# Longer VectorE operations in the state-space sections, and a step between small ScalarE products and the matmuls that read them

## The chip, the cores and the metric

One core of a Trainium2 chip runs the whole kernel, from inputs in HBM to the output in HBM. The metric is the device time of one execution in microseconds, the median of three runs. An execution of which a profile was taken gives the trace.

## What is computed

Two transformer blocks with batch 1, 256 tokens, width 2048, all in float32. The change touches the first block:

```python
mod = cond @ w_ada[i] + b_ada[i]
shift1, scale1, gate1, shift2, scale2, gate2 = jnp.split(mod, N_MOD, axis=-1)
h = _modulate(_rms(x, norm1_w[i]), shift1, scale1)
u, q, k, v = jnp.split(h @ w_in[i], splits, axis=-1)
y_ssm = _s5_mixer(u, ...)              # 64 groups of 64 complex states, a scan over 256 tokens
y_att = _dilated_attention(q, k, v, ...)
x = x + gate1 * (jnp.concatenate([y_ssm, y_att], axis=-1) @ w_out[i])
h2 = _modulate(_rms(x, norm2_w[i]), shift2, scale2)
x = x + gate2 * ((silu(h2 @ w_ffn_gate[i]) * (h2 @ w_ffn_up[i])) @ w_ffn_down[i])
```

The mixer's recurrence is h[t] = abar h[t-1] + bu[t] with complex abar for each state. y_ssm is then y * sigmoid(y @ w_glu). The second block (two attentions, a memory attention and an FFN) is not touched.

## The kernel before

**Weight tiles.** Every weight matrix comes as tiles of 128 x 4 x 512 floats (1 MB) over SP's queue (L199). Float32 products are made of three reduced ones: split_half takes a half tile apart into h (ScalarE, L207) and the residual l (VectorE, L208), and mm3 multiplies (L221, L222, then L226 with l): 24 matmuls of 512 columns a tile. The rows of w_ada come as tiles too; each is reduced with cond by one long VectorE operation (L948).

**The order.** The program order is written out by hand, and every engine works its instructions off in that order. Flow.run goes through the list of tiles. It splits tile n+1, gives tile n to main(), which makes its matmuls, and then calls step() once. step() advances every side task to its next yield (a task with rate 3: three yields). So one step is one weight tile, and what a task issues in a step stands on its engines behind the matmuls of tile n. Where main() needs something that no task has made yet, until() makes steps without tiles.

**The side tasks of the first block.** s_prep makes the tables of the state-space sections. params() computes powers of abar (E8, eight powers for all 32 pairs of groups, by three doublings in double()). Then prep(s) for each of eight sections of four pairs: the products X (L627, L635) and C, their transposes xt, the 64 powers E of the section (a copy of E8's part, L676, and three doublings, L609 to L612), the diagonal dI (L682); a section waits until section s-2 has been run. finish() multiplies out T and makes the section ready. s_run runs up to two ready sections at a time, in steps: input matmuls S and a product with E (L721 to L727), eight scans of 64 elements, one for each part and pair (L732), a product with E (L734 to L737), the output matmuls and gelu (L741 to L747), transposes (L750). When all sections are through, s_run makes glu_acts, which the w_glu tiles read. s_heads1 runs the eight attention heads; the w_out tiles read these, w_out's part 2 heads 0 to 3 before the four w_glu tiles, part 3 heads 4 to 7 behind them.

s_norm1 scales x by its rms (scaled(), L978) and in the same step transposes and modulates it: modulate() calls chunks() with ab, where ScalarE writes h (L262) and f (L263) for each chunk of 128 and VectorE the residual (L264). norm2 uses the same path with another transpose (L240). ada_end makes the gates: four ScalarE products of the identity build a diagonal (L960), a matmul with ones spreads it over the rows (L962), ScalarE copies the row (L964), and then the same again for the second diagonal of the call. There are four such calls, two for gate 2 and two for gate 5.

Of the kernel before, what the change touches and what calls it, by code (L numbers as in the profile page):

```python
# [10 lines left out]
F32 = mybir.dt.float32  # L11
F32R = mybir.dt.float32r
AF = mybir.ActivationFunctionType
OP = mybir.AluOpType
# [9 lines left out]
SP = 4  # L24
# [126 lines left out]
class Core:  # L151
# [94 lines left out]
    def chunks(self, src, n=4, w=None, ab=None, dg=None):  # L246


        nc = self.nc
        out = []  # L250
        for k in range(0, n, 2):
            ps = self.tr4(src, k, dg)
            h, l = self.acts2()
            if w is None and ab is None:
                self.split(ps, h, l)
            for j in range(2):
                if w is not None:
                    self.split(ps[:, j], h[:, j], l[:, j], w(k + j))
                elif ab is not None:
                    a, b = ab(k + j)  # L260
                    f = self.up.tile([128, 256], F32, name=self.nm("f"), tag="f", bufs=3)
                    nc.scalar.activation(h[:, j], ps[:, j], AF.Identity, scale=a, bias=b)  # L262
                    nc.scalar.activation(f, ps[:, j], AF.Identity, scale=a, bias=b)  # L263
                    nc.vector.tensor_tensor(l[:, j], f, h[:, j].bitcast(F32), op=OP.subtract)  # L264
                out.append((h[:, j], l[:, j]))
        return out

# [171 lines left out]
class Ssm:  # L439
    def __init__(self, k, a, pool):  # L440
        self.k, self.a, self.pool = k, a, pool
        nc = k.nc
        self.p = pool.tile([128, 4, 32], F32, name="ssm_p")
        nc.sync.dma_start(self.p, a["ssm_p"])
        self.i32 = pool.tile([128, 32], F32, name="i32")
        nc.gpsimd.tensor_copy(self.i32, k.ident[:, 0:32])
        for q in range(1, 4):
            nc.gpsimd.tensor_tensor(self.i32, self.i32, k.ident[:, 32 * q:32 * q + 32], op=OP.add)
        self.X = pool.tile([128, 2, SP, 4, 32], F32, name="X")
        self.C = [pool.tile([128, 2, SP, 5, 32], F32, name=f"C{i}") for i in range(3)]  # L450
        for t in [self.X] + self.C:
            nc.gpsimd.memset(t, 0.0)
        self.sec = {}
        self.done = self.complete = -1
        self.late = None

    def params(self):

        k, nc = self.k, self.k.nc
        V = nc.vector  # L460
# [133 lines left out]
        yield  # L594
        G = nc.gpsimd
        self.E8 = self.pool.tile([128, 2, 32, 8], F32, name="E8")
        G.memset(self.E8[:, 0, :, 0:1], 1.0)
        G.memset(self.E8[:, 1, :, 0:1], 0.0)
        self.double(self.E8, slice(0, 32), (0, 1, 2))
        yield  # L600

    def double(self, E, pr, steps):

        G, m = self.k.nc.vector, E.shape[2]
        for i in steps:
            n = 1 << i
            u, v = [self.small(2 * m * n).rearrange("p (i a b) -> p i a b", i=2, a=m) for _ in range(2)]
            b = [x[:, pr].unsqueeze(1).unsqueeze(3).to_broadcast([128, 2, m, n]) for x in self.ph[i]]
            G.tensor_tensor(u, E[:, :, :, 0:n], b[0], op=OP.mult)  # L609
            G.tensor_tensor(v, E[:, :, :, 0:n], b[1], op=OP.mult)  # L610
            G.tensor_tensor(E[:, 0, :, n:2 * n], u[:, 0], v[:, 1], op=OP.subtract)
            G.tensor_tensor(E[:, 1, :, n:2 * n], u[:, 1], v[:, 0], op=OP.add)  # L612

    def small(self, n=256):
        return self.pool.tile([128, 256], F32, name=self.k.nm("v"), tag="v32", bufs=4)[:, :n]

    def prep(self, s):
# [55 lines left out]
            A.activation(xt[i], ps, AF.Copy)  # L673
        yield
        E = k.unit((128, 2, SP, 64))
        A.activation(E[:, :, :, 0:8], self.E8[:, :, pr], AF.Copy)  # L676
        self.double(E, pr, (3, 4))
        yield
        self.double(E, pr, (5,))
        yield  # L680
        dI = self.small(SP * 32).rearrange("p (a b) -> p a b", a=SP)
        G.tensor_tensor(dI, self.i32.unsqueeze(1).to_broadcast([128, SP, 32]),  # L682
# [29 lines left out]
    def run(self, s, u4, ytok):  # L712
# [13 lines left out]
        V.tensor_tensor(a[:, 0], a[:, 0], b[:, 1], op=OP.add)  # L726
        V.tensor_tensor(a[:, 1], a[:, 1], b[:, 0], op=OP.subtract)  # L727
        yield
        for i in range(2):
            for q in range(SP):  # L730
                m = self.m4[:, s * SP + q:s * SP + q + 1].to_broadcast([128, 64])
                V.tensor_tensor_scan(b[:, i, q], m, a[:, i, q], initial=0.0, op0=OP.mult, op1=OP.add)  # L732
        yield
        V.tensor_tensor(a, b, eb[0], op=OP.mult)  # L734
        V.tensor_tensor(c, b, eb[1], op=OP.mult)
# [20 lines left out]
def build(ctx, tc, A, out):  # L756
    nc = tc.nc
# [195 lines left out]
    def ada_end(i, half):  # L953
        if i in gate:
            yield
            for j in range(2):
                d = (unit if i == 2 else unit2)((128, 4, 128))
                for c in R4:
                    n = 8 * half + 4 * j + c
                    S.activation(d[:, c], k.ident, AF.Copy, scale=md[i][:, n:n + 1])  # L960
                ps = k.pm()
                PE.matmul(ps, k.ones, d.rearrange("p a b -> p (a b)"), start=True, stop=True)  # L962
                row = (unit if i == 2 else unit2)()
                S.activation(row, ps, AF.Copy)  # L964
                gate[i].append(row)
            return
        yield
        if i in (1, 4):
# [19 lines left out]
    def s_norm1():  # L988
# [13 lines left out]
        for g in R4:  # L1002
            xs = scaled(g, r1)
            x[g] = [None, None]
            while (0, g // 2) not in got or (1, g // 2) not in got:
                yield
            acts1[g] = modulate(xs, g, 0)
            yield
# [626 lines left out]
```

## Time and profile before

| | |
|---|---|
| runs | 2713.55, 2709.04, 2713.08 us, median 2713.08 |
| profiled execution | 2711.92 us, span 2710.1 us |
| TensorE busy | 2616.3 us, 97% |
| VectorE busy | 1670.5 us, 62%, 2124 instructions |
| ScalarE busy | 1269.8 us, 47%, 1818 instructions |
| GpSimd busy | 98.6 us, 4% |
| HBM | 213 GB/s over the span |

Busy time is the union of an engine's instructions. Instructions of one engine overlap in the trace: the next one starts before the last one has ended, so that the distance between two starts is shorter than a duration. An idle time is put down to the instruction whose end released the waiting one. Shares over the whole span mix stages that differ, so the rows below are given by stage.

### The profile page before, as it was taken

To read this page: it belongs to the slowest core of one execution; us is meant where nothing else is said; L and a number is where in the kernel's file an instruction comes from. 1 tells how busy PE (TensorE), PEld (TensorE's weight loads), DVE (VectorE), ACT (ScalarE), POOL (GpSimd) and SP (SyncE) were. 2 spreads that over 40 slices of the span, in tenths; PEclk is the share of its full clock that TensorE was granted. 3 is DMA by queue.
4 is the path that set the end of the run, shared out by engine and by line. 5 is a ranking of instruction groups with operands and counts; after the bars stand their busy time and mean duration, and the time that the engine had idled before them with its cause. 6 is when DMAs were issued, how large, how long until landed. Compare 5 with 4: busy or idle time off the path is not lost.

```text
span 2710.1 us, 31194 instructions
## 1 busy us (share of the span) xinstructions
PE 2616.3 (97%) x12144; PEld 2171.3 (80%) x12144; DVE 1670.5 (62%) x2124; ACT 1269.8 (47%) x1818; POOL 98.6 (4%) x103
## 2 busy tenths in 40 slices
PE   8889989888999999999999999999999999999998
PEld 6778777776877888888888878888888888888887
DVE  7987999878766554554465454655554544455445
ACT  5465446553644344433445554555544433443434
POOL 2000000100000000000000021100000000000001
PEclk9999999999999999999999999999999999999999
DMA  8988765667676555555545434454455555555552
GB/s 348 362 289 328 307 244 215 253 225 297 256 277 232 200 196 190 186 194 195 186 168 192 171 130 162 166 200 171 178 215 197 186 189 196 191 186 186 187 198 96
DMA packets 90147, 578.98 MB, mean 214 GB/s; under 512 B 10000, under 2 KB 12432, under 8 KB 22672
## 3 DMA queue, kind: packets, MB, share of 16 engines
q1 hardware_dynamic: 80928, 561.61, 55.8%
q10 hardware_dynamic: 9072, 15.38, 1.7%
q8 instruction: 95, 1.56, 0.2%
q14 instruction: 52, 0.43, 0.0%
HBM read 570.67 MB, written 6.29 MB: 213 GB/s over the span
## 4 chain that ended last, share of the span: by engine, by line
PE 79%; DVE 15%; ACT 2%; issue 2%; DMA 1%; POOL 0%; ACTq 0%; DVEq 0%; POOLq 0%
PE g L226 24%; PE g L221 24%; PE g L222 24%; DVE l L208 4%; DVE r L948 4%; PE m L238 2%; DVE v L627 1%; ACT h L207 1%; DVE C L635 0%; PE m L342 0%; PE m L1484 0%; PE m L1471 0%; DVE u L732 0%; PE m L240 0%; PE m L226 0%
## 5 line engine op out<-in xcount | busy, mean ns | idle before, releaser
L208 DVE TENSOR_TENSOR l<-r,h 128x1024 fp32r<-128x1024 f32 x866 | 1028.5, 1223 | 573.6 <-ACT h L207 568.0
L221 PE MATMUL g<-h,u 128*128 128x512 f32 x3424 | 1352.6, 395 | 8.8 <-ACT h L207 6.5
L222 PE MATMUL g<-h,u 128*128 128x512 f32 x3424 | 1338.2, 391 | 0.0
L207 ACT ACTIVATE h<-r 128x1024 fp32r<-128x1024 f32 x866 | 884.1, 1056 | 625.1 <-PE g L222 593.0
L226 PE MATMUL g<-l,u 128*128 128x512 f32 x3424 | 922.2, 391 | 33.0 <-DVE l L208 33.0
L226 PEld LDWEIGHTS g<-l,u 128*128 128x128 f32 x3424 | 643.2, 189 | 178.3 <-DVE l L208 45.6
L221 PEld LDWEIGHTS g<-h,u 128*128 128x128 f32 x3424 | 647.9, 189 | 144.8 <-ACT h L207 10.2
L222 PEld LDWEIGHTS g<-h,u 128*128 128x128 f32 x3424 | 648.0, 189 | 132.4 <-issue 1.0
L948 DVE CUSTOM_DVE_ANT_0 r<-r,cond,vec 128x2048 f32<-128x2048 f32 x96 | 224.5, 2343 | 0.2
L271 ACT ACTIVATE u<-m 128x512 fp32r<-128x512 f32 (+1 forms) x80 | 42.7, 574 | 164.1 <-PE m L238 128.3
L272 DVE TENSOR_TENSOR u<-m,u 128x512 fp32r<-128x512 f32 (+1 forms) x80 | 50.0, 658 | 86.6 <-ACT u L271 86.5
L291 ACT ACTIVATE j<-u 128x512 bf16<-128x512 f32 (+2 forms) x92 | 47.3, 514 | 118.2 <-DVE u L1204 31.2
L238 PE MATMUL m<-ident,u 128*128 128x128 f32 x372 | 53.4, 287 | 19.8 <-POOL base_e L488 7.1
L274 ACT ACTIVATE u<-m,vec 128x256 fp32r<-128x256 f32 x86 | 38.9, 472 | 69.8 <-PE m L342 30.8
L275 DVE SCALAR_TENSOR_TENSOR u<-m,vec,u 128x256 fp32r<-128x256 f32 x86 | 40.0, 481 | 48.2 <-ACT u L274 48.1
L238 PEld LDWEIGHTS m<-ident,u 128*128 128x128 f32 x372 | 45.9, 148 | 27.5 <-ACT u L978 8.7
L299 POOL TENSOR_TENSOR r<-s,mhalf 128x2 f32<-128x2 f32 x5 | 5.5, 1102 | 1098.7 <-DVE s L298 1098.7
L1251 DVE TENSOR_TENSOR w<-g,w 128x512 f32<-128x512 f32 x24 | 16.5, 687 | 43.1 <-PE g L226 43.1
L1235 DVE SCALAR_TENSOR_TENSOR w<-g,r,w 128x512 f32<-128x512 f32 x22 | 15.5, 747 | 44.4 <-PE g L226 44.4
L1233 DVE TENSOR_TENSOR w<-g,w 128x512 f32<-128x512 f32 x22 | 14.2, 686 | 44.3 <-PE g L226 44.3
L1507 DVE TENSOR_TENSOR u<-g,u 128x512 f32<-128x512 f32 x22 | 14.2, 686 | 44.3 <-PE g L226 44.3
L1227 ACT ACTIVATE w<-g,r 128x512 f32<-128x512 f32 x22 | 13.9, 686 | 52.9 <-PE g L226 52.9
(238 smaller groups left out, 1204.6 us busy)
## 6 DMA issues: line engine op xcount, KB each, us to landing
r<-in_w_ada_dram SPq DMA_DIRECT2D x96, 1024.0 KB, 5.6
r<-in_wg_dram SPq DMA_DIRECT2D x88, 1024.0 KB, 4.8
r<-in_wu_dram SPq DMA_DIRECT2D x88, 1024.0 KB, 4.8
r<-in_wd_dram SPq DMA_DIRECT2D x88, 1024.0 KB, 4.8
r<-in_w_in_dram SPq DMA_DIRECT2D x32, 1024.0 KB, 6.0
r<-in_w_out_dram SPq DMA_DIRECT2D x32, 1024.0 KB, 4.8
r<-in_w_qkv_dram SPq DMA_DIRECT2D x24, 1024.0 KB, 4.8
r<-in_w_xk_dram SPq DMA_DIRECT2D x16, 1024.0 KB, 9.0
```

What stands on the lines that cost most here:

```text
L207: nc.scalar.activation(h, r, AF.Copy)
L208: (nc.gpsimd if shared else nc.vector).tensor_tensor(l, r, h.bitcast(F32), op=OP.subtract)
L221: nc.tensor.matmul(ps[t][:, :n], al[:, s], h[:, k], start=first and k == 0, stop=False)
L222: nc.tensor.matmul(ps[t][:, :n], ah[:, s], h[:, k], start=False, stop=False)
L226: nc.tensor.matmul(ps[t][:, :n], ah[:, s], l[:, k], start=False, stop=last and k == len(acts) - 1)
L238: self.nc.tensor.transpose(o, i, self.ident)
L271: nc.scalar.activation(h, ps, AF.Copy)
L272: nc.vector.tensor_tensor(l, ps, h.bitcast(F32), op=OP.subtract)
L274: nc.scalar.activation(h, ps, AF.Copy, scale=w)
L275: nc.vector.scalar_tensor_tensor(l, ps, w, h.bitcast(F32), op0=OP.mult, op1=OP.subtract)
L291: self.nc.scalar.activation(j[:, :n], src, AF.Square, accum_out=acc)
L948: V.tensor_tensor_reduce(r, r, cond, 1.0, v("b_ada", 8 * h + j), OP.mult, OP.add, md[h // 2][:, n:n + 1])
```

## The change

The residual of the modulated chunks is taken for two chunks at once, so f is a pair tile of the common pool. A second table F8 holds the powers 0, 8, ..., 56, and outer() makes a section's E from E8 and F8 with six operations in one step, where a copy and three doublings stood in two steps. The eight scans of a section become one over 512 elements, with a tile of decay factors that is zero at the start of each part (filled once) and that ScalarE writes in front of each scan. The gate diagonals of one call are both built first, a step apart, and the matmuls follow in later steps. scaled() gets a step of its own.

```diff
@@ chunks
+            f = None
+            if ab is not None:
+                f = self.unit((128, 2, 256))
             for j in range(2):
...
-                    f = self.up.tile([128, 256], F32, name=self.nm("f"), tag="f", bufs=3)
                     nc.scalar.activation(h[:, j], ps[:, j], AF.Identity, scale=a, bias=b)
-                    nc.scalar.activation(f, ps[:, j], AF.Identity, scale=a, bias=b)
-                    nc.vector.tensor_tensor(l[:, j], f, h[:, j].bitcast(F32), op=OP.subtract)
+                    nc.scalar.activation(f[:, j], ps[:, j], AF.Identity, scale=a, bias=b)
+                    if j:
+                        nc.vector.tensor_tensor(l, f, h.bitcast(F32), op=OP.subtract)
@@ Ssm.__init__
+        self.decay = [pool.tile([128, 2, SP, 64], F32, name=f"decay{i}") for i in range(2)]
-        for t in [self.X] + self.C:
+        for t in [self.X] + self.C + self.decay:
             nc.gpsimd.memset(t, 0.0)
@@ params
-        G.memset(self.E8[:, 0, :, 0:1], 1.0)
-        G.memset(self.E8[:, 1, :, 0:1], 0.0)
-        self.double(self.E8, slice(0, 32), (0, 1, 2))
-        yield
-
-    def double(self, E, pr, steps):
+        self.F8 = self.pool.tile([128, 2, 32, 8], F32, name="F8")
+        for i, t in enumerate((self.E8, self.F8)):
+            G.memset(t[:, 0, :, 0:1], 1.0)
+            G.memset(t[:, 1, :, 0:1], 0.0)
+            self.double(t, slice(0, 32), 3 * i)
+            yield
+
+    def double(self, E, pr, first):
...
+    def outer(self, E, pr):
+
+        V = self.k.nc.vector
+        f = lambda t, i, d: t[:, i, pr].unsqueeze(d).to_broadcast([128, SP, 8, 8])
+        u, v = [[self.small().rearrange("p (a m n) -> p a m n", a=SP, m=8) for _ in range(2)] for _ in range(2)]
+        for i in range(2):
+            V.tensor_tensor(u[i], f(self.E8, i, 2), f(self.F8, 0, 3), op=OP.mult)
+            V.tensor_tensor(v[i], f(self.E8, 1 - i, 2), f(self.F8, 1, 3), op=OP.mult)
+        for i in range(2):
+            V.tensor_tensor(E[:, i].rearrange("p a (m n) -> p a m n", m=8), u[i], v[i],
+                            op=OP.add if i else OP.subtract)
@@ prep
         E = k.unit((128, 2, SP, 64))
-        A.activation(E[:, :, :, 0:8], self.E8[:, :, pr], AF.Copy)
-        self.double(E, pr, (3, 4))
-        yield
-        self.double(E, pr, (5,))
+        self.outer(E, pr)
         yield
@@ run
-        for i in range(2):
-            for q in range(SP):
-                m = self.m4[:, s * SP + q:s * SP + q + 1].to_broadcast([128, 64])
-                V.tensor_tensor_scan(b[:, i, q], m, a[:, i, q], initial=0.0, op0=OP.mult, op1=OP.add)
+        d = self.decay[s % 2]
+        nc.scalar.activation(d[:, :, :, 1:64], self.m4[:, s * SP:s * SP + SP].unsqueeze(1).unsqueeze(3)
+                             .to_broadcast([128, 2, SP, 63]), AF.Copy)
+        flat = lambda t: t.rearrange("p i a n -> p (i a n)")
+        V.tensor_tensor_scan(flat(b), flat(d), flat(a), initial=0.0, op0=OP.mult, op1=OP.add)
         yield
@@ ada_end
             yield
+            d = [(unit if i == 2 else unit2)((128, 4, 128)) for _ in range(2)]
             for j in range(2):
-                d = (unit if i == 2 else unit2)((128, 4, 128))
                 for c in R4:
                     n = 8 * half + 4 * j + c
-                    S.activation(d[:, c], k.ident, AF.Copy, scale=md[i][:, n:n + 1])
+                    S.activation(d[j][:, c], k.ident, AF.Copy, scale=md[i][:, n:n + 1])
+                yield
+            for j in range(2):
                 ps = k.pm()
-                PE.matmul(ps, k.ones, d.rearrange("p a b -> p (a b)"), start=True, stop=True)
+                PE.matmul(ps, k.ones, d[j].rearrange("p a b -> p (a b)"), start=True, stop=True)
                 row = (unit if i == 2 else unit2)()
                 S.activation(row, ps, AF.Copy)
                 gate[i].append(row)
+                yield
             return
@@ s_norm1
             xs = scaled(g, r1)
             x[g] = [None, None]
+            yield
             while (0, g // 2) not in got or (1, g // 2) not in got:
                 yield
             acts1[g] = modulate(xs, g, 0)
```

## Rows read from the trace of the kernel before

**Rows 1.** Stages: window, us, busy PE, PEld, DVE, ACT, POOL, clock, DMA, GB/s.

```profile
0.00:176.00 176.00, 151.36 (x680) 119.85 (x680) 156.37 (x295) 88.21 (x140) 23.63 (x25) 1.00 0.93 351
176.00:300.00 124.00, 118.48 (x542) 98.25 (x542) 95.74 (x112) 68.31 (x96) 0.01 (x1) 0.96 0.80 312
300.00:543.00 243.00, 217.44 (x1152) 183.11 (x1152) 227.97 (x450) 129.65 (x285) 17.66 (x10) 0.94 0.63 241
543.00:562.40 19.40, 12.22 (x68) 10.54 (x66) 13.67 (x29) 13.84 (x32) 0.00 (x0) 0.82 0.53 193
...
700.00:2710.00 2010.00, 1992.55 (x9144) 1658.11 (x9142) 1064.14 (x1103) 899.78 (x1151) 56.65 (x67) 1.00 0.52 190
```

**Rows 2.** TensorE's waits over the span: us in total, times, longest us.

```profile
PE g L226 <- DVE l L208: 33.0, 29, 3.4
...
PE m L238 <- ACT u L978: 7.0, 5, 2.6
...
PE m L962 <- ACT w L960: 3.7, 2, 1.9
```

**Rows 3.** VectorE's timeline, tables and one section's E: start, us, instruction, count.

```profile
109.58 0.27 DVE L609 TENSOR_TENSOR v<-E,q 128x64 f32<-128x64 f32 x1
...
112.57 2.34 DVE L948 CUSTOM_DVE_ANT_0 r<-r,cond,vec 128x2048 f32<-128x2048 f32 x1
...
337.71 0.21 DVE L609 TENSOR_TENSOR v<-u,csl 128x64 f32<-128x64 f32 x1
...
340.56 0.28 DVE L682 TENSOR_TENSOR v<-i,ssm_p 128x128 f32<-128x128 f32 x1
```

**Rows 4.** VectorE's timeline, products of one section and the scans of the next.

```profile
310.53 0.68 DVE L734 TENSOR_TENSOR u<-u,u 128x512 f32<-128x512 f32 x1
311.13 0.68 DVE L735 TENSOR_TENSOR u<-u,u 128x512 f32<-128x512 f32 x1
...
312.19 0.42 DVE L737 TENSOR_TENSOR u<-u,u 128x256 f32<-128x256 f32 x1
312.53 1.56 DVE L732 TENSOR_TENSOR_SCAN u<-m,u 128x64 f32<-128x64 f32 x8
314.00 0.86 DVE L1037 STREAM_TRANSPOSE u<-u 128x128 f32<-128x128 f32 x4
```

**Rows 5.** ScalarE's groups up to 700 us: count, busy us, mean ns, idle before.

```profile
L688 ACT ACTIVATE u<-X 128x512 f32<-128x512 f32 x16 | 9.1, 617 | 0.0
```

**Rows 6.** TensorE's timeline, first transposes of the scaled rows, with the idle time before.

```profile
176.81 0.47 PE L238 MATMUL m<-ident,u 128*128 128x128 f32 x1 [2.40 <-ACT u L978]
...
191.77 0.33 PE L238 MATMUL m<-ident,u 128*128 128x128 f32 x1 [2.57 <-ACT u L978]
```

**Rows 7.** Two windows behind those gaps, columns as in rows 1.

```profile
176.80:183.10 6.30, 6.15 (x18) 4.99 (x19) 4.66 (x10) 5.30 (x11) 0.00 (x0) 0.50 0.89 324
193.70:196.90 3.20, 3.20 (x9) 2.42 (x9) 1.41 (x4) 3.20 (x8) 0.00 (x0) 0.50 0.01 5
```

**Rows 8.** The page's groups, VectorE: count, busy us, mean ns, idle before.

```profile
L208 DVE TENSOR_TENSOR l<-r,h 128x1024 fp32r<-128x1024 f32 x866 | 1028.5, 1223 | 573.6 <-ACT h L207 568.0
...
L948 DVE CUSTOM_DVE_ANT_0 r<-r,cond,vec 128x2048 f32<-128x2048 f32 x96 | 224.5, 2343 | 0.2
```

**Rows 9.** VectorE's groups up to 700 us, the residuals of modulated chunks.

```profile
L264 DVE TENSOR_TENSOR u<-f,u 128x256 fp32r<-128x256 f32 x32 | 13.4, 425 | 27.5 <-ACT f L263 27.4
```

**Rows 10.** Timeline, the last section's product and the first w_glu matmul.

```profile
542.21 0.68 DVE L734 TENSOR_TENSOR u<-u,u 128x512 f32<-128x512 f32 x1
...
562.35 0.99 PE L221 MATMUL g<-h,u 128*128 128x512 f32 x1
```

**Rows 11.** TensorE's timeline, the second diagonal of a gate call for gate 5.

```profile
774.28 1.12 PE L962 MATMUL m<-w,ones 128*128 128x512 f32 x2 [1.85 <-ACT w L960]
```

**Rows 12.** VectorE's waits from 290 to 545 us: us, times, longest us.

```profile
DVE u L724 <- PE m L721: 9.2, 3, 4.9
```

**Rows 13.** ScalarE's timeline, the copies of one section's transposed X.

```profile
466.49 1.09 ACT L673 ACTIVATE u<-m 128x512 f32<-128x512 f32 x2 [2.57 <-PE m L672]
```

More of the change, by code (lines that the diff above doesn't have):

```diff
@@ L596, in params @@
         self.E8 = self.pool.tile([128, 2, 32, 8], F32, name="E8")
-        G.memset(self.E8[:, 0, :, 0:1], 1.0)
-        G.memset(self.E8[:, 1, :, 0:1], 0.0)
-        self.double(self.E8, slice(0, 32), (0, 1, 2))
-        yield
-    def double(self, E, pr, steps):
+        self.F8 = self.pool.tile([128, 2, 32, 8], F32, name="F8")
[5 more added lines that the diff above has]
+    def double(self, E, pr, first):
         G, m = self.k.nc.vector, E.shape[2]
-        for i in steps:
+        for i in range(3):
             n = 1 << i
             u, v = [self.small(2 * m * n).rearrange("p (i a b) -> p i a b", i=2, a=m) for _ in range(2)]
-            b = [x[:, pr].unsqueeze(1).unsqueeze(3).to_broadcast([128, 2, m, n]) for x in self.ph[i]]
+            b = [x[:, pr].unsqueeze(1).unsqueeze(3).to_broadcast([128, 2, m, n]) for x in self.ph[first + i]]
             G.tensor_tensor(u, E[:, :, :, 0:n], b[0], op=OP.mult)
```

## The prediction, made before the changed kernel was run

> **What bounds the kernel now.** I read the stages first [rows 1], then who kept TensorE waiting [rows 2]. From 700 us on TensorE is busy 1992.55 of 2010 us: there only work taken from TensorE, or a gap in it, counts. In front of that the kernel is bound by VectorE: up to 176 us it is busy 156.37 us (most of the rest is the start), from 300 to 543 us 227.97 of 243 us, while TensorE has 25.6 us of idle time there. TensorE's largest wait in the whole span is for VectorE's residual of a weight half, 33.0 us [rows 2]. Between 176 and 300 us VectorE has slack and TensorE's gaps are chains of short operations; from 543 to 562.4 us no weight tile runs and TensorE has 12.22 us of side work at a mean clock of 0.82. So an edit on VectorE is priced by the distance between starts (not by durations, which overlap) where VectorE is full, an edit at TensorE by the gap that it closes.
>
> **The tables E8 and F8.** The twelve operations that make E8 take from 109.58 to 112.57, 3.0 us [rows 3]. F8 is the same set again: +3.0 us, at about 112 us, where VectorE is full, so all of it is on the path. In each section the three doublings take from 337.71 to 340.56, 2.85 us [rows 3]; six operations of 128x256 replace them. Such operations start 0.34 us apart (312.19 to 312.53 for L737 [rows 4]), 6 x 0.34 = 2.05, about 2.1 with the wait of the first sum for its products: -0.75 us a section. Sections 0 and 1 do this before 176 us (-1.5, so with F8 that stretch gets 1.5 longer), sections 2 to 7 in the full stretch: **-4.5**. Bounds: 6 x 0.42 if the starts don't overlap, then -2.0; I stay with the starts.
>
> **The scan.** Eight scans of 64 elements occupy 312.53 to 314.00, 1.47 us, 0.184 each [rows 4]. One of 512 is not in the trace. Between plain operations of 256 and 512 elements the starts go from 0.34 to 0.60 us [rows 4], 1.04 ns an element and 0.07 to begin. If all that the scan has more is its beginning, 512 elements cost 0.65 us; if nothing of it is, 1.47 and nothing is won. I take the beginning of the plain operation: (0.184 - 0.07) / 64 = 1.8 ns an element, 512 x 1.8 + 0.07 = 1.0 us. Saved 0.47 a section, eight sections: **-3.8** (0 to -6.6). [...]
>
> **The decay tile.** It adds one ScalarE copy of 128x504 a section, about 0.61 us by the 0.617 of a copy of 128x512 with a repeated input [rows 5], and E's small copy goes. ScalarE is busy 129.65 of 243 us [rows 1], so its time is free. But the scan now waits for ScalarE, and behind the scan on VectorE stand the next row product and the next two weight residuals, for which TensorE waits. I take 0 for this; the price if it fails is the slower rival. The fills on GpSimd for the new tiles stand at the start; it is busy 23.63 of the first 176 us [rows 1]: 0.
>
> **Scaled rows.** The two scalings of a group and the transposes that read them are now a step, that is a weight tile, apart. Before, TensorE waited 2.40 us at 176.81 and 2.57 at 191.77 for the scalings [rows 6]; of the 7.0 us in five waits [rows 2] the other 2.0 are 0.3 right behind the second and 1.7 at 262 us. [...] So 2.40 + 2.57 + 0.3 + 4.75 = 10.0 us at 176 to 200 us. I do not keep all of it. VectorE arrives 1.5 us later (F8, above), and in this place it now does both X products of section 2 in one step: an ada row of 2.3 us, two residuals that start 1.15 apart, and eight operations of some 0.42 make 7.9 us for this tile, where TensorE's 24 matmuls of a tile take 5.2 (1992.55 us over 9144 matmuls [rows 1]; the VectorE rows [rows 8]); 2.7 us of wait come back. 10.0 - 1.5 - 2.7 = 5.8, so **-6** with F8 in it (0 to -9), and **-1.5** at 262 us (0 to -1.7). What is late next: the weight stream, DMA share 0.80 over this stretch [rows 1].
>
> **One residual for two chunks.** 16 operations of 128x512 replace 32 of 128x256. Where VectorE is late this saves 16 x 0.07 us, where it waits for ScalarE the pair ends 0.27 us later; it did wait, 27.4 us in all in front of the 32 [rows 9]. Four calls lie in 176 to 270 us and four at 677 to 697 us, both times beside matmuls that are already fed. 0 (-1.1 to +2.2).
>
> **Fewer steps.** The main loop makes one step of all side tasks per weight tile, and a section's preparation takes three yields per step. It had nine yields, now it has eight. Counting the yields of each task for the kernel before, the SSM sections end three steps after the main loop has reached the first w_glu tile, and the trace has just this: the last row product starts at 542.21 and the first w_glu matmul at 562.35 [rows 10]. For the changed kernel the count gives a section every three steps (before: three and four in turn), so that all sections are done one step before that tile is reached: this wait goes. But the last attention heads do not move; now the loop waits two steps for them four tiles later, at the first w_out tile that reads them. So the stall is not lost but moved. Before it costs 19.4 - 12.22 us of idle time and half of the slow 0.36 of the stretch, 3.5: 10.7 us [rows 1]. Two steps of three leave 7.1, so 3.6 are won. Against that, section 7's products and transposes, 2.1 + 0.6 us of VectorE, move out of the stall into the full stretch. Net **-0.9** (-8 if the heads run hidden beside the w_glu tiles, +3 if the new wait is as long as the old).
>
> **Gate diagonals.** In the first gate event after 700 us TensorE waits 1.85 us at 774.28 for the second diagonal, which ScalarE could only begin after copying the first row [rows 11]; the second event has the same, 3.7 us in all [rows 2], where TensorE is full. With both diagonals built steps ahead these go: **-3.7**. The first two events lie in stretches where VectorE is late anyway: 0 (-3.7 at most).
>
> **The sum.** -6 - 1.5 - 4.5 - 3.8 - 0.9 - 3.7 = -20.4 us against the profiled execution's 2711.92 us (span 2710.1), which is 1.2 below the median of 2713.08 and inside the runs' spread: 2691.5, I say 2691.
>
> **Rivals.** (a) *The denser sections turn TensorE into the bound.* In 300 to 543 us TensorE is busy 217.44 us, only 10.5 less than VectorE [rows 1]. At one section per three steps, the block that finishes a section, the output matmuls of the one before and the input matmuls of the next fall in one step every time. Where that happened before, VectorE waited for TensorE, 9.2 us in three places [rows 12]. Five or six such places instead of three, at 3 us, give back 6 to 9 us of the 8.3; for it: section 7 has no products of a next section to cover the wait; against it: the middle sections have 3.4 us of them. Result about 2700.
> (b) *The weight stream is next in 176 to 300 us*, so that closing those gaps brings nothing: 2698.5. Against it: its share is 0.80 [rows 1], so there is time to catch up.
> (c) *Both at once, or the stall only moves and grows*: 2691.5 + 7.5 + 8.3 = 2707, no change that can be told.
> (d) *Slower: the scan waits for ScalarE.* The decay copy stands in ScalarE's queue behind copies of the same step that wait for TensorE: the transposed X waited 2.57 us at 466.49 [rows 13]. If ScalarE is later than VectorE at that place, all eight scans take the delay, and the residuals behind them. From 20.4 / 8 = 2.6 us per section on nothing is left; at 4 us it is 32 us and the time 2691.5 + 32 = 2723. Against it: VectorE has an ada row and two residuals, 4.6 us [rows 8], between ScalarE's place and its own. That the long scan costs what eight short ones do is in the bounds above, not a case of its own.
>
> **How the numbers follow.** Forecast 0.54, (a) 0.16, (b) 0.07, (c) 0.12, (d) 0.11. Faster by over 0.2% (5.4 us, about what a measurement of this kernel can tell from no change) are the forecast, (a) and (b): 0.77; same 0.12, slower 0.11. Low end: all bounds on the good side, -9 - 1.7 - 4.5 - 6.6 - 8 - 7.4 = -37: 2675. High end: the forecast's poor ends and (c), 2708. Outside are (d) and a little of each tail.
>
> **What would show it.** Right: no wait of TensorE for L978 or for the diagonals' copies, and no stretch at half clock at 177 to 183 us; VectorE still over 90% busy from 300 us to the first w_glu tile, that stretch 5 to 10 us shorter; the w_glu tiles following the w_out tiles without a break, and a new, shorter break four tiles later; a long scan of 0.9 to 1.1 us. Wrong: idle time of VectorE before the scan put down to ScalarE; idle time before L724 well over 9.2 us; TensorE waiting for residuals as long as before; a break before the heads as long as 19 us.

## The result and the profile after

Four runs of the changed kernel gave 2691.46, 2688.58, 2687.30 and 2689.22 us, median 2688.9, beside a median of 2712.93 for the kernel before: ratio 0.9918, 95% interval 0.9907 to 0.9930, so 19 to 25 us less. The forecast was 2691. The profiled execution took 2691.46 us, its span is 2689.7.

The two kernels have the same 433 weight tiles in the same order, and each tile has eight L221 matmuls, so the start of every eighth L221 matmul in TensorE's timeline says how far either kernel is. What grows between two such marks is lost, what shrinks is won:

```
tile (first L221 matmul)             before     after   after-before   step   forecast
xk22, the 11th tile                   78.73     77.57       -1.2       -1.2   (no change there)
xv13, in front of norm1              168.16    169.12       +1.0       +2.1   +1.5 (F8, two sections)
u0.0, first w_in tile                232.94    226.13       -6.8       -7.8   -7.5 (scaled rows, without F8)
u1.3                                 285.88    281.55       -4.3       +2.5   -1.5
k4.0, the full stretch begins        305.86    301.54       -4.3        0
o0p3, first w_out tile of part 3     589.45    571.33      -18.1      -13.8   -9.2 (E, scans, steps)
o0p0, behind part 3                  618.56    597.08      -21.5       -3.4    0 (gate 2)
first FFN tile                       679.76    661.48      -18.3       +3.2    0
behind both gate 5 calls             890.60    868.41      -22.2       -3.9   -3.7
last tile                           2695.68   2675.12      -20.6       +1.6    0
```

The first 1.2 us are no effect: kernels that change nothing ahead of 300 us (the gates alone and the scan alone, below) were 0.9 and 1.2 us earlier at that tile, and 2.1 and 0.7 at k4.0. One execution tells a tile's place to about 1 us, and less well where TensorE's clock fell at other places (last section).

The stages of after, cut at these marks (window, us, busy PE, PEld, DVE, ACT, POOL, clock, DMA, GB/s), for [rows 1]:

```profile
169.10:226.10 57.00, 54.61 (x257) 44.57 (x256) 52.06 (x57) 32.26 (x48) 2.73 (x1) 1.00 0.94 349
226.10:301.50 75.40, 73.03 (x337) 60.19 (x336) 55.58 (x68) 39.67 (x54) 0.00 (x0) 0.98 0.80 314
301.50:528.70 227.20, 208.50 (x1162) 176.18 (x1160) 218.44 (x354) 128.87 (x282) 17.66 (x10) 0.97 0.66 249
528.70:551.40 22.70, 22.58 (x110) 18.21 (x109) 17.96 (x27) 18.32 (x38) 0.00 (x0) 1.00 0.70 262
551.40:571.30 19.90, 12.17 (x59) 9.55 (x58) 14.70 (x23) 13.27 (x24) 0.00 (x0) 0.77 0.57 211
```

And the same stages of before, cut at the same tiles:

```profile
168.20:232.90 64.70, 58.99 (x257) 48.16 (x256) 54.67 (x66) 32.91 (x48) 2.73 (x1) 0.92 0.84 322
232.90:305.90 73.00, 71.29 (x338) 59.22 (x337) 54.66 (x76) 38.60 (x52) 0.00 (x0) 1.00 0.79 310
305.90:562.30 256.40, 223.66 (x1189) 188.63 (x1188) 235.77 (x462) 141.59 (x315) 17.66 (x10) 0.93 0.62 235
562.30:583.90 21.60, 21.60 (x107) 18.30 (x105) 11.21 (x16) 10.81 (x21) 0.00 (x0) 0.93 0.26 98
583.90:589.40 5.50, 5.50 (x26) 4.55 (x25) 5.50 (x8) 2.80 (x4) 0.00 (x0) 1.00 0.92 355
```

From k4.0 to the first w_glu tile 256.4 us became 227.2: the break in front of w_glu is gone. The first three w_glu tiles took 22.7 us, before 21.6. The fourth, with the new break behind it, took 19.9 us where it took 5.5, with the clock at 0.77; so the break itself is 14.4 us long.

The stretches of [rows 7] are now at full clock, though TensorE has done more by then:

```profile
176.80:183.10 6.30, 6.30 (x39) 5.55 (x37) 6.14 (x11) 3.90 (x6) 0.00 (x0) 1.00 1.00 394
193.70:196.90 3.20, 3.20 (x14) 2.67 (x15) 3.20 (x2) 0.75 (x1) 0.00 (x0) 1.00 0.85 333
```

VectorE's timeline answers [rows 3] and [rows 4]: the long scan (L748) up to the next start, and the six operations of outer() up to the operation behind them:

```profile
297.43 1.22 DVE L748 TENSOR_TENSOR_SCAN u<-decay,u 128x512 f32<-128x512 f32 x1
298.57 0.66 DVE L739 TENSOR_TENSOR u<-m,u 128x512 f32<-128x512 f32 x1
...
332.73 0.42 DVE L626 TENSOR_TENSOR v<-E,F 128x256 f32<-128x256 f32 x1
...
334.74 0.28 DVE L697 TENSOR_TENSOR v<-i,ssm_p 128x128 f32<-128x128 f32 x1
```

1.14 us for a scan (forecast 1.0, eight short ones 1.47) and 2.01 us for an E (forecast 2.1, before 2.85). The scans start 1.10 to 1.14 us ahead of the operation behind them, the last but one aside, whose next operation had to wait. No idle time stands before any of the eight scans. TensorE's waits, us in total, times, longest, for [rows 2]: those for L978 and L960 have no answer any more, while the wait for weight residuals is no shorter:

```profile
PE g L226 <- DVE l L208: 34.8, 32, 2.7
```

### The profile page after: what moved, and what is told of

The parts are those of the page before. It is cut to its first block, busy times and chain, and to the rows that moved or that the text cites. A ratio compares the mean times of both kernels' runs of the same rounds, so it can differ in the third digit from the quotient of the medians.

```text
span 2689.7 us, 31097 instructions
## 1 busy us (share of the span) xinstructions
PE 2609.1 (97%) x12144; PEld 2164.5 (80%) x12144; DVE 1663.0 (62%) x2016; ACT 1270.9 (47%) x1818; POOL 101.0 (4%) x107
## 4 chain that ended last, share of the span: by engine, by line
PE 80%; DVE 14%; ACT 3%; issue 2%; DMA 1%; POOL 0%; ACTq 0%; DVEq 0%; POOLq 0%
PE g L226 25%; PE g L221 25%; PE g L222 24%; DVE l L208 4%; DVE r L964 4%; PE m L238 2%; DVE v L645 1%; ACT h L207 1%; PE m L345 0%; PE m L1504 0%; PE m L1491 0%; PE m L240 0%; DVE C L653 0%; DMA r<-in_w_ada_dram 0%; PE m L226 0%
## 5 line engine op out<-in xcount | busy, mean ns | idle before, releaser
L221 PE MATMUL g<-h,u 128*128 128x512 f32 x3424 | 1352.5, 395 | 8.2 <-ACT h L207 5.0
L226 PE MATMUL g<-l,u 128*128 128x512 f32 x3424 | 920.9, 391 | 34.8 <-DVE l L208 34.8
L221 PEld LDWEIGHTS g<-h,u 128*128 128x128 f32 x3424 | 646.7, 189 | 146.0 <-ACT h L207 9.2
```

Source lines behind the costliest of these rows:

```text
L221: nc.tensor.matmul(ps[t][:, :n], al[:, s], h[:, k], start=first and k == 0, stop=False)
L226: nc.tensor.matmul(ps[t][:, :n], ah[:, s], l[:, k], start=False, stop=last and k == len(acts) - 1)
```

## The experiments

All ratios are to the kernel before, run on the same chip, with 95% intervals.

**The scaled rows alone.** Edit: the one new line in s_norm1.

```diff
             xs = scaled(g, r1)
             x[g] = [None, None]
+            yield
```

> The kernel before with the step between the scaled rows and their transposes alone. If the sum of the prediction holds for this part by itself: 2.40 + 2.57 + 0.3 us of waits and 4.75 us of half clock at 176 to 200 us go, 2.7 come back, 1.5 more go at 262 us, with no F8 in front: about 9 us less (2704), and in the trace no wait of TensorE for the scaled rows. If instead the weight stream gives part of it back (in the kernel after, a weight tile at 270 us came 4.4 us late, when VectorE had stood 6.4 us for modulated chunks and no weight buffer was freed): about 5 us less (2708), with that late tile in this trace too.

Measured: 2704.77 us, ratio 0.9976 (0.9966 to 0.9986), 6.5 us less, between the two theories. By tiles it is 8.8 us ahead of before at u0.0 (the gates alone, which change nothing there, are 2.1 ahead too), 11.8 at q2.1, and 8.2 at u1.3, four tiles on, and from there to the end: 3.5 us are given back. So closing the gaps pays, and something behind it takes part of it back.

**One residual or two.** Edit, in after: each modulated chunk gets its own f and its own residual again, as in the kernel before.

```diff
-                    if j:
-                        nc.vector.tensor_tensor(l, f, h.bitcast(F32), op=OP.subtract)
+                    nc.vector.tensor_tensor(l[:, j], f, h[:, j].bitcast(F32), op=OP.subtract)
```

> The kernel after with one residual for each modulated chunk, as before. The prediction took 0 for that edit, -1.1 to +2.2. In the trace of after the tile behind norm2 came 1.3 us later than before it did, and VectorE stood 15.0 us for the copies of modulated chunks around 176 to 300 us in front of weight residuals. If the merged residual costs there: 1 to 4 us less than after (2685 to 2688 where after has 2689). If it costs nothing: the same as after, and the tile behind norm2 is as late.

Measured: 2685.91 us, ratio 0.9911 (0.9898 to 0.9925); the interval overlaps with that of after. By tiles it is 0.3 us ahead of after at q2.1, 2.2 at u1.3 and 3.4 at the end. The 1.9 us from q2.1 to u1.3 lie at one tile. Its windows, of after, of this run, and of the run with outer() on GpSimd (below), which has two residuals as well:

```profile
266.20:276.10 9.90, 7.53 (x26) 5.70 (x26) 9.90 (x10) 4.77 (x5) 0.00 (x0) 0.83 0.79 275
```

```profile
265.90:273.90 8.00, 5.88 (x26) 4.51 (x26) 8.00 (x9) 4.53 (x5) 0.00 (x0) 1.00 0.79 294
```

```profile
268.40:278.00 9.60, 7.50 (x26) 5.62 (x25) 9.60 (x10) 4.58 (x6) 0.00 (x0) 0.82 0.81 310
```

TensorE is idle for 2.37, 2.12 and 2.10 us. The rest of the difference is its clock, which is granted at 0.83, 1.00 and 0.82 on the mean: the third run has the low one with two residuals. So the merged residual costs some 0.3 us here; that it brings the low clock too is not shown. The tile behind norm2 was as late as in after, so that part of the expectation was wrong; its lateness is a matter of the clock (0.89 in that stretch of after, last section).

**The merged residual alone.** Edit, in before: the part of the change in chunks().

> The kernel before with one residual for two modulated chunks alone. The prediction took 0 (-1.1 to +2.2). From the comparison in the kernel after (one residual for each chunk was some 2 to 3 us better, 2.2 of it at the tiles behind the third group of norm1): 1 to 3 us more than before (2713), with tiles at 264 to 280 us late. Rival, the merged residual costs only where the scaled rows are a step ahead: no difference.

Measured: 2709.94 us, ratio 0.9999 (0.9990 to 1.0007), and from u0.0 to the end it stays 2.0 to 2.3 us ahead of before (one tile at 340 us apart), as the gates alone did up to the gates. The rival said no difference, and there is none; that the merged residual costs more than the 0.3 us above where the scaled rows stand a step ahead is not shown.

**What gives back.** SP's timeline of after around that place, the same of before, then VectorE's of after with TensorE's wait (start, us, instruction, idle before it):

```profile
244.10 0.33 SPq L199 DMA_DIRECT2D r<-in_w_ada_dram  x1
256.64 0.33 SPq L199 DMA_DIRECT2D r<-in_w_in_dram  x1
```

```profile
250.89 0.33 SPq L199 DMA_DIRECT2D r<-in_w_ada_dram  x1
263.44 0.33 SPq L199 DMA_DIRECT2D r<-in_w_in_dram  x1
```

```profile
250.50 0.69 DVE L267 TENSOR_TENSOR u<-u,u 128x512 fp32r<-128x512 f32 x1 [6.43 <-ACT u L265]
...
262.46 0.69 DVE L267 TENSOR_TENSOR u<-u,u 128x512 fp32r<-128x512 f32 x1 [2.73 <-ACT u L265]
...
264.89 2.35 DVE L964 CUSTOM_DVE_ANT_0 r<-r,cond,vec 128x2048 f32<-128x2048 f32 x1
267.16 2.35 DVE L964 CUSTOM_DVE_ANT_0 r<-r,cond,vec 128x2048 f32<-128x2048 f32 x1
269.43 2.35 DVE L208 TENSOR_TENSOR l<-r,h 128x1024 fp32r<-128x1024 f32 x2
270.71 1.20 PE L226 MATMUL g<-l,u 128*128 128x512 f32 x4 [2.37 <-DVE l L208]
```

For 12.5 us no weight load is issued, since the residuals and ada rows that would free weight buffers stand on VectorE behind its waits. But before has the same stop, as long, and no late tile behind it; so the stop is not what costs. VectorE stands 6.4 and 2.7 us in its queue for copies of modulated chunks, whose transposes stand in TensorE's queue behind a weight tile. Behind the second wait come two ada rows of 2.3 us, then the residual of a weight half, and TensorE waits 2.4 us for that. The tile is 4.4 us late; the low clock behind the wait (0.83 in the window above) is most of the rest. To test this, the scaled rows of the last group are made while the group before it still waits for its ada halves, so that its transposes and residuals come one tile earlier:

```diff
         for g in R4:
+            if g not in xs:
+                scale(g)
+                yield
             while (0, g // 2) not in got or (1, g // 2) not in got:
+                if g == 2 and 3 not in xs:
+                    scale(3)
                 yield
```

> The kernel after with two residuals, and the scaled rows of the last group of norm1 made while the group before it still waits for its ada halves; its transposes and residuals then stand one weight tile earlier. Theory of what was given back at 264 to 276 us: no weight load is issued from 243.9 to 256.4 us in the trace of after, since the buffers' readers stand on VectorE behind residuals of modulated chunks that wait for transposes (5.5 and 1.8 us), and three ada rows then come at once in front of a weight tile's residuals. With the second of these waits a tile earlier the stop is shorter and the tile at 270 us comes up to 3.5 us earlier: 2682 to 2685 where the run with two residuals has 2686. Rival, the stop stays as long, it only begins with both groups at once: within 1 us of that run, or later.

Measured: 2683.69 us, ratio 0.9900 (0.9884 to 0.9917), 2.2 us less than the run with two residuals, though the intervals overlap. By tiles it is 0.7 us behind that run at q2.1, 2.6 ahead at u1.3 and 1.2 at the first w_glu tile. The late tile is gone; TensorE is not idle in it:

```profile
265.60:271.30 5.70, 5.70 (x26) 4.45 (x26) 5.70 (x7) 2.18 (x3) 0.00 (x0) 1.00 1.01 411
```

The first two residuals of the last group now run without a wait:

```profile
256.16 0.91 DVE L264 TENSOR_TENSOR u<-f,u 128x256 fp32r<-128x256 f32 x2
```

SP's stop (243.73 to 256.27 us there) is as long as before, so the part of the expectation on it was wrong (and its 5.5 and 1.8 us are the waits of the run with two residuals); what went is the second stand of VectorE, so that the ada rows and the weight residual behind it come earlier. This is the fastest kernel of the study.

**A step less, alone.** Edit, in before: the doublings of E in one step, no operation changed.

```diff
-        self.double(E, pr, (3, 4))
-        yield
-        self.double(E, pr, (5,))
+        self.double(E, pr, (3, 4, 5))
         yield
```

> The kernel before with the doublings of a section's E in one step instead of two, no operation changed: eight steps of preparation instead of nine, and nothing else. The prediction's theory: the three-step wait at the first w_glu tile becomes a two-step wait at the first w_out tile of part 3, about 1 us less (2712). Rival, step count is the larger part of the gain: 8 us less or more (2705). Rival, denser sections only make TensorE wait: 3 us more (2716).

Measured: 2716.87 us, ratio 1.0023 (1.0013 to 1.0032): 6 us slower. It reached the first w_glu tile 19.7 us ahead of before, and the tile behind the new break 3.4 us behind it. TensorE's timeline at the end of that break shows why (start, us, instruction, idle before it; L960 is here the matmul that spreads a gate diagonal):

```profile
587.90 2.04 PE L960 MATMUL m<-u,ones 128*128 128x512 f32 x2 [3.89 <-DVE u L272]
...
591.80 2.07 PE L960 MATMUL m<-u,ones 128*128 128x512 f32 x2 [1.85 <-ACT u L958]
...
592.88 1.41 PE L221 MATMUL g<-h,u 128*128 128x512 f32 x1
```

A gate 2 call falls into the moved wait, and its matmuls stand in TensorE's queue ahead of the w_out tile, each for its own chain of short operations. Two of them take 2.04 and 2.07 us there; at a clock of 1.00 two took 1.12 [rows 11]. Over the w_glu tile and the break together the clock is 0.73 (window below).

**outer() and F8 alone.** Edit, in before: the parts of the change in params(), double(), outer() and prep(), with the step less that goes with them.

> The kernel before with F8 and outer() alone, so with the step less in each preparation. By the prediction's terms: +3.0 for F8, -0.75 in each of eight sections, the moved stall -0.9: about 4 us less (2709). If the number of steps carries more than its share (rival: the stall in front of the first w_glu tile goes and the new one is much shorter): 10 us or more less (2703 or below). If VectorE's gain is lost to TensorE in the denser sections: within 1 us of before.

Measured: 2709.93 us, ratio 0.9996 (0.9987 to 1.0004). It has the same break, 29 us long. Beside the run before it, the same steps with the shorter E give 7 us, though F8 is paid; but by itself this part of the change brings nothing that can be told.

**The gate diagonals alone.** Edit, in before: the part of the change in ada_end().

> The kernel before with the gate diagonals alone. The prediction: the two waits of 1.85 us at 774 and 867 us go, 3.7 us less (2709). Rival, the longer chain of steps or the extra diagonals meet another wait behind them: 0 to 2 us less. From 700 us on no other tile of the trace should move.

Measured: 2705.88 us, ratio 0.9980 (0.9972 to 0.9989), 5.4 us less. By tiles it is 5.7 us ahead at the end: 4.1 of it lie at the two gate 5 calls, and about 1 behind the gate 2 calls; 2.1 stand ahead of 300 us, where it changes nothing, and 1.6 are lost at the tile of w_uq where after loses it too.

**Both together.** Edit, in before: the last two edits, to see whether they add up.

> The kernel before with F8 and outer() (a step less in each preparation) and the gate diagonals together. Theory formed from the traces of the two parts alone: with the step less, the wait of the loop moves to the first w_out tile of part 3, and there the four matmuls of a gate 2 call stand in TensorE's queue in front of the tile and wait for their diagonals (2.0 + 3.9 + 1.9 us, at half clock); with the diagonals a step ahead these matmuls come behind the tile. So the two parts give more together than apart: 1.3 + 5.4 + some 9, about 15 us less than before (2696). Rival, they add up: 6 to 7 us less (2704.5).

Measured: 2693.48 us, ratio 0.9938 (0.9926 to 0.9951): 17 us less, where the sum of the two is 6.5. The windows of the break, first with the step less alone, then with outer() and gates:

```profile
563.80:592.90 29.10, 16.06 (x63) 10.96 (x61) 20.28 (x30) 16.58 (x34) 0.00 (x0) 0.73 0.66 251
```

```profile
558.30:578.20 19.90, 12.17 (x59) 9.54 (x57) 14.70 (x23) 13.26 (x24) 0.00 (x0) 0.78 0.56 211
```

The 9.2 us between them are the gate matmuls with their waits: with the diagonals a step ahead they come behind the weight tile. (Over the four w_glu tiles and the break together it is 7.5 us.) This break is the same, to 0.1 us, as that of after. So three quarters of the gain come from these two edits, and 10 of their 17 us only from their being together.

**The scan alone.** Edit, in before: the parts of the change in run() and for the decay tiles.

> The kernel before with the long scan and its decay tile alone. The prediction took 0.47 us a section, 3.8 us in all (2707.5); the trace of after has the long scan at 1.10 to 1.14 us from start to start, against 1.44 to 1.48 for the eight, so 8 x 0.34 = 2.7 us less (2708.5) if all of it is on the path. Rival, the scan waits for ScalarE here: no gain, and idle time of VectorE before it put down to the decay copy. Rival, TensorE takes the gain back: within 1 us of before.

Measured: 2707.59 us, ratio 0.9987 (0.9979 to 0.9996), 3.5 us less. No scan waits for ScalarE here either: 0.0 us of idle time in front of the eight.

**The rest of the break.** Is the new break a reserve? Edit, in after, the order of the last w_in tiles:

```diff
-    LATE = (("k", 4), ("v", 6), ("v", 7), ("q", 3), ("k", 5), )
+    LATE = (("k", 4), ("v", 6), ("k", 5), ("q", 3), ("v", 7), )
```

> The kernel after with another order of the last w_in tiles: k of the second half ahead of q, v of the second half at the end, since v is ready for the heads one step after its tile and k three. No work is added or taken. By the count of steps heads 4 to 7 then start two steps earlier and are done when the first w_out tile of part 3 is reached, so the break of 19.9 us there goes. If that break is idle time and half clock that can be filled: 8 us less than after or more (2681). Rival, the heads' chains then stand beside the last sections in the stretch where VectorE is full, and TensorE waits there instead: within 2 us of after (2689).

Measured: 2691.26 us, ratio 0.9929 (0.9915 to 0.9942), no better than after. The break is gone (6.1 us for that tile, at full clock), but the first w_glu tile came 12 us later than in after:

```profile
540.50:564.90 24.40, 24.40 (x115) 19.87 (x115) 17.22 (x27) 18.00 (x37) 0.00 (x0) 0.93 0.57 214
564.90:571.00 6.10, 6.10 (x33) 5.15 (x31) 6.10 (x8) 3.04 (x5) 0.00 (x0) 1.00 0.85 314
```

The heads' work stood in the break because it has to stand somewhere: VectorE is busy for 14.70 of its 19.9 us. Moved forward, it stands in the stretch where VectorE has no room (busy for 218.44 of 227.2 us in after), and TensorE has new waits there, for a residual on VectorE and for copies of a section's transposes (us, times, longest, from 430 to 541 us):

```profile
PE m L1121 <- DVE u L275: 3.9, 1, 3.9
PE m L238 <- ACT u L691: 3.7, 1, 3.7
```

**VectorE's work to GpSimd.** The six operations of outer() on GpSimd, which is busy for 17.66 of the 227.2 us of that stretch in after, in the run with two residuals:

```diff
-        V = self.k.nc.vector
+        V = self.k.nc.gpsimd
```

> The kernel after with two residuals (as the run before) and the six operations of outer() on GpSimd instead of VectorE, with four buffers of their own. The theory that VectorE's work is what the sections pay with: 2.01 us less on VectorE in each of six sections of the full stretch, so 8 to 12 us less than with two residuals (2675 to 2678), and weight tiles up to 1.5 us earlier in each section. Rival, VectorE's other operations get slower beside GpSimd's, or the section waits for GpSimd: the same or more (2686 or above), with longer VectorE operations or idle time put down to GpSimd.

Measured: 2692.57 us, ratio 0.9932 (0.9919 to 0.9946), about 6 us more than without it (0.9911). VectorE's groups from 295 to 526 us (count, busy us, mean ns, idle before), first with outer() on VectorE, then on GpSimd, and GpSimd's own:

```profile
L208 DVE TENSOR_TENSOR l<-r,h 128x1024 fp32r<-128x1024 f32 x51 | 60.2, 1221 | 1.0 <-ACT h L207 1.0
L642 DVE TENSOR_TENSOR v<-u,pi 128x256 f32<-128x256 f32 x12 | 5.0, 418 | 0.0
```

```profile
L208 DVE TENSOR_TENSOR l<-r,h 128x1024 fp32r<-128x1024 f32 x50 | 60.5, 1251 | 0.7 <-ACT h L207 0.7
L643 DVE TENSOR_TENSOR v<-u,pi 128x256 f32<-128x256 f32 x12 | 6.4, 533 | 0.0
...
L627 POOL TENSOR_TENSOR u<-o,o 128x256 f32<-128x256 f32 x12 | 14.2, 1203 | 64.3 <-DVE u L1108 33.5 <-PE m L734 24.2 <-PE m L715 6.6
```

An operation of 0.42 us on VectorE takes 0.8 to 1.2 on GpSimd on average, and VectorE's products beside it grow from 418 to 533 ns. A weight residual grows from 1221 to 1251 ns, a long scan from 1196 to 1249; the first product that reads the input matmuls' m does not (688 and 687), nor does the transpose of y (290 and 289). What makes some of them longer was not shown. By tiles the run is 4.2 us behind the one with two residuals at k4.0 (1.6 of it the low clock shown above), and 7.9 at the first w_glu tile. From 300 to 528 us VectorE is busy for 219.18 of 228.0 us, with outer() on VectorE from 300 to 525.5 us for 217.83 of 225.5: 36 operations left it, and it is as full as with them, since others of its operations became longer.

And the same with v of the second half as the last w_in tile:

> The run with outer() on GpSimd, and v of the second half as the last w_in tile as well. In the kernel after that order moved the heads' work out of the break into the stretch where VectorE is full and gave nothing. If VectorE's work is the limit there, room made on VectorE lets part of it pay: 2 to 5 us less than with outer() on GpSimd alone. Rival, something else holds that stretch (transposes and copies in TensorE's queue): no difference, within 1.5 us.

Measured: 2697.21 us, ratio 0.9949 (0.9937 to 0.9961). With outer() on GpSimd costing instead of saving, the run could not show what it was made for; the order of tiles lost another 4.6 us.

## Why the prediction was right

The time is 2 us from the forecast, and most of the mechanisms it named are in the trace. But the tiles are off by more than that in both directions: +4.0 us at 262 us, -4.6 in the sections, -3.4 behind part 3, +3.2 and +1.6 where no term stood. That these cancel to 2 us is luck.

- **F8 and E: right.** E went from 2.85 to 2.01 us a section (forecast -0.75 each, measured -0.84), and up to xv13 the change costs 2.1 us (forecast 1.5).
- **Scan: mechanism right, gain too large.** I took the beginning of a plain operation as all that a long scan saves, 1.0 us. It is 1.10 to 1.14, so 0.34 a section and 2.8 us for eight, instead of 3.8. With 0.07 us to begin, that is 2.0 to 2.1 ns an element where I had 1.8; what the scan spends it on is not shown.
- **Decay tile, rival (d): fell.** Idle time of 0.0 us before all scans, in after and in the scan alone. The copy ended 2.4 to 12.7 us ahead of its scan in after. What covers it is not always what the forecast named: ada rows and weight residuals stood between in four of the eight, in the other four only products of a section being prepared and transposes.
- **Scaled rows, first two: right.** -7.8 us from xv13 to u0.0, without F8's share, against -7.5; the clock of 0.50 behind 176.8 and 193.7 us is 1.00 now. Some 1.2 us of that are chance: the gates alone and the scan alone change nothing there and gain that much on the profiled execution of before, whose clock was 0.92 in this stretch. No run shows the 4.75 us in the forecast's sum as a time by itself. What the runs show in its place is 9.5 us at a clock of 0.50 [rows 7], of which it takes half, and, in TensorE's timeline of before, matmuls that start 0.43 us apart in the first of these windows, where behind it, at 0.98 from 183.1 to 193.7 us, they start 0.23 apart:

```profile
180.69 0.63 PE L221 MATMUL g<-h,u 128*128 128x512 f32 x1
181.12 0.63 PE L222 MATMUL g<-h,u 128*128 128x512 f32 x1
...
183.72 0.39 PE L221 MATMUL g<-h,u 128*128 128x512 f32 x1
183.95 0.39 PE L222 MATMUL g<-h,u 128*128 128x512 f32 x1
```

- **Scaled rows at 262 us: wrong, -1.5 forecast, +2.5 measured.** The wait of 1.7 us for L978 went, but three tiles on TensorE now waits 2.4 us for a weight residual, and the clock falls (0.83 at that tile). What is late next was mis-named. I looked at the load of the weight stream (0.80) and found room; it was VectorE, which works off two ada rows ahead of that residual. Rival (b) was near in place, not in cause. With two residuals, where the clock at that tile is 1.00, this stretch is 0.6 us longer than in before instead of 2.5, and as much with the scaled rows alone; so some 2 of the 4.0 us are the step that failed. The rest I put down to the clock; the scan alone, which has the waits of before there, loses 1.6 us in this stretch too. The merged residual, costed at 0 with bounds to +2.2, is shown to cost 0.3 us here, and 0 by itself.
- **Fewer steps: place right, price wrong.** The w_glu tiles follow without a break and a break stands four tiles later, as the count said. But two prices failed. The cost did not shrink from 10.7 to 7.1 us: the window of the break and the w_glu tile in it has 7.7 us of idle time, and by the same measure for the slow share, (1 - 0.77) x 19.9 = 4.6 us of low clock (0.50 from 563 to 571 us), 12.3 in all. Its length, 14.4 us, stayed under the 19 that were named as a sign of being wrong. And a gate 2 call falls into it, which I had put into stretches "where VectorE is late anyway" at 0. Without the gate edit the step less makes the kernel 6 us slower, outside the bounds (+3 at most); with it, outer() and gates give 17 us. That joint effect was in no term.
- **The sections as a whole: -13.8 us from k4.0 to o0p3 against -9.2.** The windows give VectorE 252.5 busy us of 283.5 before and 251.1 of 269.8 after. The shorter scans and E's in that stretch are some 7 us by their starts, but one more ada row, one more weight residual and two w_glu products fell into it; what went is idle time of VectorE, 31.0 to 18.7 us. So the gain there is fewer breaks more than less work. On TensorE idle time went from 32.7 to 26.5 us in these windows, and busy time from 250.8 to 243.3, which I put down to the clock: from k4.0 to the first w_glu tile it is 0.93 in before and 0.97 in after. The forecast had priced the clock in the breaks only, at nothing in the sections; the busy time is about half of the 13.8. The sign that it named for the full stretch holds: 227.2 us, VectorE busy for 96% of it, where before takes 237.1 up to its break at 543 us.
- **Rival (a): small.** VectorE waited 4.2 us in three places for the section's input matmuls (L736 of after) where [rows 12] had 9.2 in three, so there were no more such places, and shorter ones. TensorE's waits for residuals from 300 us to the first w_glu tile fell from 14.8 to 11.1 us; that the total stayed (34.8 against 33.0, [rows 2]) is due to 4.9 us, instead of 0.3, from 165 to 300 us, 2.4 of them at the late tile. As a sign for or against the forecast, the total was badly chosen.
- **Gates for gate 5: right.** -3.9 us for the two calls, forecast -3.7 (-4.1 in the gates alone); TensorE's matmuls for the spread wait no more (count, busy us, mean ns, idle before):

```profile
L980 PE MATMUL m<-w,ones 128*128 128x512 f32 x8 | 4.1, 592 | 0.0
```

What stays open: the last 2 to 5 us, and what brings the low clock at one place and not at another. The single edits were told apart to about 2 us each, and the tile marks of one execution to about 1 where the clock is the same.

## What to carry to other kernels

Two edits that put small work into the same place have to be priced there together: a gap that is moved takes with it whatever else is queued at its new place, and here a chain of four matmuls, on which the gates alone save about 1 us where it stood, cost 7 to 9 us once the wait had come to it. A stop of the loads is not yet a late tile: 12.5 us without a load cost nothing in before. When a tile is late, look at what TensorE waited for and at what stood ahead of that in its engine's queue; here it was two ada rows of 2.3 us ahead of one residual. And before taking a break of TensorE for a reserve, look at who is busy in it: here VectorE was, for 14.70 of 19.9 us, and filling 14 us of break from a stretch in which VectorE was full gave nothing (2691.26 us beside 2688.9).

## What the runs showed of the hardware

The same idle gap does not always cost the same clock. Before one w_uq tile both kernels leave TensorE idle for 2.00 us, for the same reason. Of after, the window with the gap and the next:

```profile
1518.00:1521.00 3.00, 1.00 (x7) 0.68 (x6) 0.00 (x0) 3.00 (x7) 0.00 (x0) 1.00 0.67 284
1521.00:1524.00 3.00, 3.00 (x9) 2.37 (x8) 1.54 (x2) 2.98 (x4) 0.00 (x0) 0.54 0.00 0
```

and of before:

```profile
1540.00:1543.00 3.00, 1.00 (x8) 0.72 (x7) 0.00 (x0) 3.00 (x7) 0.00 (x0) 1.00 0.72 300
1543.00:1546.00 3.00, 3.00 (x15) 2.47 (x14) 1.33 (x2) 2.98 (x5) 0.00 (x0) 1.00 0.00 0
```

In after the clock is 0.54 in the window behind the gap and 0.89 in the 3 us behind that, 1.7 us by these windows (the last step of the table is 1.6); in before it stays at 1.00. The gates alone lose 1.6 us at this tile too; the fastest kernel, with the same 2.0 us of idle time there from 1509 to 1515 us, has 1.00 in every window of 3 us from 1506 to 1521. From o0p0 to the first FFN tile after lost 3.2 us: its clock is 0.89 over 64.4 us, where before has 0.97 over 61.2, with about the same idle time (10.3 and 10.8 us). From 615 to 620 us after leaves TensorE idle for 2.0 us, and the clock is 0.51 and 0.81 in the next two windows of 5 us; the fastest kernel leaves it idle for 2.3 us from 611 to 616 us and has 1.00 in the next two. And at the late tile of w_in, shown above, idle times of 2.12 and 2.10 us left the clock at 1.00 in one kernel and brought 0.82 in the other. So some 5 us of a comparison of these kernels can be of this kind (an estimate, 1.6 + 3.2 of the above), and what decides it was not settled.
